# Pairs of the HGRN heads on column strips of the array, and a delta rule whose keys are transposed once for a pair of heads

## The chip, the cores and the metric

The kernel runs on one core of a Trainium2 chip. The metric is the device time of one execution in microseconds, from repeated runs. The profile is of one further execution. Its engines are PE (the matrix engine, TensorE), PEld (its weight loads), DVE (VectorE), ACT (ScalarE), POOL (GpSimd) and SP, which here only issues DMAs.

## What is computed

One layer of a diffusion backbone over 512 latent tokens and 256 context tokens of width 1024: a modulated norm, one input projection, two token mixers in parallel, their merge, an output projection, and a SwiGLU block. The change touches the two mixers. Both run in two directions over chunks of tokens:

```
# mixer A, gated delta rule, per chunk (u solved from a triangular system before)
u_c    = u_c - w_c @ s
s_next = gam_end * s + k_end.T @ u_c              # k_end = k * exp(g_end - g)
o      = (q * exp(g)) @ s + att @ u_c
# mixer B, HGRN2, per chunk
pair   = exp(lg[i] - lg[j])  for j <= i, else 0   # a decay per channel k
att_ij = sum_k q[i,k] * k[j,k] * pair[i,j,k]
o      = (q * exp(lg)) @ s + att @ v
```

## The kernel before

All matmuls of the wide projections are split in three products of rounded halves (line 110, a helper `mm3`; the halves `hi` and `lo` are made by ACT at line 100 and DVE at line 102). The order of all instructions on each engine is fixed when the program is built: a list `PLAN` says in which order steps of six streams are written down (two pairs of delta rule heads `G0` and `G2`, four HGRN heads `H0` to `H3`), with pieces of independent work between them (`F`, gate projections into `pgate`, and sums for the modulation), and a scheduler then interleaves them by priority. The rest of the gate projections is written behind the streams at a low priority, so that PE has it to fill gaps and to do at the end. Then come the up projections (`pup`), the output projection (`pwo`), and the SwiGLU block (`pf`, `pfo`).

**HGRN head (`hgrn`).** The decay of a pair in a chunk of 128 tokens can't be taken apart into a factor for i and one for j without overflow. So the pairs are split in a diagonal and seven levels b = 1, 2, 4, ... 64: at level b a pair is one whose two tokens lie in neighbouring halves of a block of 2b tokens. For each level `kq` holds scaled keys and queries (ACT lines 511 and 512, DVE line 513), and `att` (line 488) multiplies them for all 128 x 128 pairs of each of the 4 chunks into a PSUM bank `pA`; DVE (line 493) then copies only the pairs of that level into the matrix `AT`, by a mask `lev`. For the diagonal (level 7 in the code) ACT copies the whole product (line 491). K and L are moved on to the next level by DVE at lines 515 and 516. `AT` is used in the head's output `h_po`.

**Delta rule pair (`gdn_pair`).** Two heads (index e) are worked on together. A triangular system is solved in blocks of 32 and 64 (tiles `p_pR`, `p_pY`, `p_pX`, `p_pRb`, `p_pYb`, which are themselves matmuls on parts of the array), with `T1`, `T2` and `X64` as scratch in three buffers of the tag `blk`. Then six steps run over the chunks, with four independent states (two heads, two directions), each step in a PSUM bank `pk` out of three banks of the tag `ga`. A unit (one step of one state) is: keys times state (line 789), remainder `r` (DVE line 790), times the solved matrix (792), the update u = that product scaled by `nbkv` (ACT line 794), queries times state (796, latent chunks only), the transposed keys (799, PE against the identity) scaled by their decay to the end of the chunk into `ke` (ACT line 800), `ke` times u (801) into the new state (ACT line 804 in the first step, DVE line 806 later), and the output (810, ACT 815, DVE 813 and 816).

A product of 32-bit floats appears as two records on PE (two passes); a transposition against the identity as one. The products of rounded halves appear as one.

## Time and profile before

| | |
|---|---|
| time, median of 3 runs | 1084.16 us (1082.39 to 1086.25) |
| profiled execution, its own time | 1081.61 us |
| profiled execution, span from first to last instruction | 1079.6 us |
| mean granted TensorE clock | 0.990 of full |
| PE busy in the span | 1014.1 us (94%) |
| DVE busy | 656.5 us (61%) |
| ACT busy | 554.5 us (51%) |

The two mixers fill the span from about 100 to 580 us. The four heads make their pairs near 266 to 294, 345 to 386, 449 to 478 and 544 to 563 us, and the two pairs of delta rule heads step from 285.6 to 330.6 and from 471.2 to 513.5 us. A row of the timeline gives the start of a group of instructions, its length, and its count; the length holds the latency of the last one, so the spacing of a stream is read from starts.

### The profile page before, as it was taken

The numbers are of one execution on the slowest core, as the hardware profiler recorded it, in microseconds if no ns is written. First come the engines' busy times: TensorE is split into PE (matmuls) and PEld (weight loads), VectorE is DVE, ScalarE is ACT, GpSimd is POOL, SyncE is SP. The second block draws the span as 40 slices with busy tenths as digits, with TensorE's granted clock in tenths as the row PEclk, the third lists the DMA queues.
The fourth block names the chain that finished last, engine by engine and source line by source line (L and its number), as shares of the span: only waits on it lengthen the run. The fifth ranks groups of instructions, "written<-read, shape, count | busy, mean of one in ns | idle before, by whom it ended". The sixth has DMA issues, their size and how long they took to land.

```text
span 1079.6 us, 16501 instructions
## 1 busy us (share of the span) xinstructions
PE 1014.1 (94%) x6455; PEld 839.9 (78%) x6455; DVE 656.5 (61%) x1238; ACT 554.5 (51%) x1042; POOL 76.6 (7%) x133
## 2 busy tenths in 40 slices
PE   4999999979999999999999899999999999999996
PEld 2686788858897877789777688797888878888785
DVE  3336886789867967976797565776343433422524
ACT  3456578748976765887774643442222222221212
POOL 1010000320002022000201000010000000000000
PEclk8999999999999999999999999999999999999999
DMA  9953412122004213200738743455333323322222
GB/s 329 290 168 91 138 55 65 54 79 59 3 11 147 64 45 88 59 2 22 241 112 280 239 159 120 137 158 174 98 97 96 96 85 98 97 97 96 86 95 95
DMA packets 134529, 122.07 MB, mean 113 GB/s; under 512 B 5533, under 2 KB 110259, under 8 KB 134451
## 3 DMA queue, kind: packets, MB, share of 16 engines
q1 hardware_dynamic: 127715, 100.20, 29.9%
q0 software_dynamic: 4640, 17.30, 4.9%
q10 hardware_dynamic: 2096, 3.50, 0.9%
q8 instruction: 51, 0.84, 0.3%
q14 instruction: 27, 0.22, 0.1%
HBM read 110.51 MB, written 10.49 MB: 112 GB/s over the span
## 4 chain that ended last, share of the span: by engine, by line
PE 60%; DVE 13%; DMA 9%; ACT 7%; issue 7%; POOL 3%; SPq 0%; POOLq 0%; ACTq 0%; DVEq 0%
PE pf L110 20%; PE pfo L110 10%; PE pg L330 3%; PE pup L110 3%; PE h_z L110 3%; PE pgate L110 2%; DMA mwb<-in_mod_w_dram 2%; DVE lo L102 2%; DMA mwe<-in_mod_w_dram 2%; PE h_zv L110 2%; DMA ug<-gdram 1%; ACT hi L100 1%; DMA gdram<-gt 1%; PE p_s_pk L801 1%; PE g_k_zl L110 1%
## 5 line engine op out<-in xcount | busy, mean ns | idle before, releaser
L100 ACT CAST hi<-raw 128x1024 fp32r<-128x1024 f32 (+1 forms) x131 | 129.7, 991 | 279.9 <-PE pf L110 97.3
L102 DVE TENSOR_TENSOR lo<-raw,hi 128x1024 fp32r<-128x1024 f32 (+1 forms) x131 | 150.5, 1150 | 172.6 <-ACT hi L100 172.2
L110 PE MATMUL pf<-hhi,lo 128*128 128x512 f32 (+1 forms) x352 | 133.8, 380 | 0.8 <-DVE lo L102 0.8
L110 PE MATMUL pf<-hhi,hi 128*128 128x512 f32 (+1 forms) x352 | 133.8, 381 | 0.0
L110 PE MATMUL pf<-hlo,hi 128*128 128x512 f32 (+1 forms) x352 | 133.7, 380 | 0.0
L110 PEld LDWEIGHTS pf<-hhi,lo 128*128 128x128 f32 x352 | 66.2, 188 | 13.7 <-DVE lo L102 1.2
L110 PEld LDWEIGHTS pf<-hlo,hi 128*128 128x128 f32 x352 | 66.2, 188 | 12.5 <-DVE hlo L1042 0.2
L110 PEld LDWEIGHTS pf<-hhi,hi 128*128 128x128 f32 x352 | 66.1, 188 | 12.5
L110 PE MATMUL pfo<-lo,uh 128*128 128x512 f32 x176 | 68.8, 391 | 0.1
L110 PE MATMUL pfo<-hi,ul 128*128 128x512 f32 x176 | 68.5, 389 | 0.0
L110 PE MATMUL pfo<-hi,uh 128*128 128x512 f32 x176 | 67.9, 390 | 0.0
L110 PE MATMUL pgate<-hhi,lo 128*128 128x512 f32 x144 | 59.2, 412 | 6.5 <-DVE lo L102 6.5
L110 PE MATMUL pgate<-hhi,hi 128*128 128x512 f32 x144 | 59.2, 411 | 2.3 <-ACT hi L100 2.3
L110 PE MATMUL pgate<-hlo,hi 128*128 128x512 f32 x144 | 58.2, 404 | 0.0
L1098 DVE TENSOR_TENSOR sg<-sg,pf 128x512 f32<-128x512 f32 x22 | 15.1, 687 | 49.3 <-PE pf L110 49.3
L835 DVE SCALAR_TENSOR_TENSOR acc<-mwb,sc,acc 128x256 f32<-128x256 f32 x72 | 34.5, 484 | 12.4 <-DMA mwb<-in_mod_w_dram 11.2
L110 PEld LDWEIGHTS pfo<-lo,uh 128*128 128x128 f32 x176 | 33.0, 188 | 7.8 <-DVE lo L102 1.0
L110 PEld LDWEIGHTS pfo<-hi,uh 128*128 128x128 f32 x176 | 32.8, 188 | 7.4 <-ACT hi L100 0.7
L110 PEld LDWEIGHTS pgate<-hhi,lo 128*128 128x128 f32 x144 | 27.8, 193 | 13.8 <-DVE lo L102 8.9
L110 PE MATMUL h_z<-hhi,hi 128*128 128x512 f32 x96 | 38.1, 397 | 0.4 <-ACT abT L376 0.3
L110 PEld LDWEIGHTS pfo<-hi,ul 128*128 128x128 f32 x176 | 33.0, 188 | 6.8
L110 PE MATMUL h_z<-hhi,lo 128*128 128x512 f32 x96 | 38.0, 396 | 0.0
(443 smaller groups left out, 2498.3 us busy)
## 6 DMA issues: line engine op xcount, KB each, us to landing
raw<-in_ffn_w_in_dram SPq DMA_DIRECT2D x44, 512.0 KB, 3.7
raw<-in_w_in_dram SPq DMA_DIRECT2D x37, 512.0 KB, 3.7
raw<-in_ffn_w_out_dram SPq DMA_DIRECT2D x22, 512.0 KB, 3.6
mwb<-in_mod_w_dram POOLq DMA_DIRECT2D x18, 512.0 KB, 4.6
mw<-in_mod_w_dram SPq DMA_DIRECT2D x16, 512.0 KB, 6.0
mwe<-in_mod_w_dram POOLq DMA_DIRECT2D x7, 1024.0 KB, 6.1
gdram<-gt SPq DMA_DIRECT2D x24, 256.0 KB, 3.3
raw<-in_w_in_dram SPq DMA_DIRECT2D x18, 256.0 KB, 2.9
```

Of the source, the lines that this page charges most:

```text
L100: nc.scalar.copy(hi[:, :, :], raw[:, :, :])
L102: nc.vector.tensor_tensor(lo[:, :, :], raw[:, :, :], hi.bitcast(F32), op=ALU.subtract)
L110: nc.tensor.matmul(ps, a[u](k), b[v](k), start=(start and n == 0), stop=(stop and n == tot - 1))
L330: nc.tensor.matmul(pg0[i][:, :], u[:, P * i:P * i + P], v[:, d, :], start=(d == 0 and n == 0), stop=(d == KT - 1 and n == 2))
L801: nc.tensor.matmul(pk[:, 2 * P:3 * P], kend[:, :], u[:, :], start=True, stop=True)
L835: nc.vector.scalar_tensor_tensor(acc[:, :], mw[:, k - k0, :], sc[:, k:k + 1], acc[:, :], op0=ALU.mult, op1=ALU.add)
L1098: nc.vector.tensor_tensor(sg[:, :], sg[:, :], pgu[1][:, :], op=ALU.mult)
```

## The change

In the HGRN heads `att` no longer multiplies 128 x 128 pairs. For the diagonal and levels b = 1 to 16, all pairs of interest lie in diagonal blocks of 32 x 32, so 4 blocks a chunk are multiplied, each on its own strip of 32 columns of the array (`tile_position` (0, 32 j); all 128 rows are used, since the sum runs over 128 channels). Level 32 multiplies each block of 32 with its neighbour, in the same way; level 64 multiplies 2 blocks of 64 a chunk on strips of 64 columns. The product of a level so is 128 x 4 x 32 numbers instead of 128 x 4 x 128 (128 x 4 x 64 at level 64). The diagonal and the first five levels gather in a small tile `AD`, by a mask cut to 32 columns; four DVE copies put it into `AT`, and levels 32 and 64, of which every pair counts, go there by four and two ACT copies, without a mask.

In the delta rule, the six blocks of keys of a head are transposed ahead of the steps, in two PSUM banks of `ga`, and copied by ACT into a tile `kt` of the tag `blk`. The decay to the chunk's end is put on the update instead of the keys: `nbe` is `nbkv` times the decay, `ue` is the product scaled by `nbe`, and `kt` times `ue` gives the new state. u itself is made only for latent chunks, where the output needs it.

```diff
-    lev = [(r // (2 * b) == c // (2 * b)) & (r // b != c // b) for b in LEVELS]
+    r, c = r % NB, c[:, 0:NB]
+    lev = [(r // (2 * b) == c // (2 * b)) & (r // b != c // b) for b in LEVELS[0:NSM]]
...
             AT = hg.tile([P, 4, P], F32, name=n + "AT", tag="AT")
+            AD = hg.tile([P, 4, NB], F32, name=n + "AD", tag="AD")

             def att(kq, lvl):
+                w = 64 if lvl == 6 else NB
                 pA = bank("ha", f"{n}pA{lvl}")
                 for c in range(4):
-                    nc.tensor.matmul(pA[:, P * c:P * c + P], kq[:, 0, P * c:P * c + P], kq[:, 1, P * c:P * c + P],
-                                     start=True, stop=True)
+                    for j in range(P // w):
+                        kt0, qt0 = P * c + w * j, P * c + w * (j ^ (lvl in (5, 6)))
+                        nc.tensor.matmul(pA[w * j:w * j + w, w * c:w * c + w], kq[:, 0, kt0:kt0 + w], kq[:, 1, qt0:qt0 + w],
+                                         start=True, stop=True, tile_position=(0, w * j))
+                pAv = pA[:, 0:4 * w].rearrange("p (c i) -> p c i", i=w)
                 if lvl == 7:
-                    nc.scalar.copy(AT[:, :, :], pA.rearrange("p (c i) -> p c i", i=P))
+                    nc.scalar.copy(AD[:, :, :], pAv)
+                elif lvl < NSM:
+                    nc.vector.copy_predicated(AD[:, :, :], lev[:, NB * lvl:NB * lvl + NB].unsqueeze(1).to_broadcast([P, 4, NB]), pAv)
                 else:
-                    nc.vector.copy_predicated(AT[:, :, :], lev[:, P * lvl:P * lvl + P].unsqueeze(1).to_broadcast([P, 4, P]),
-                                              pA.rearrange("p (c i) -> p c i", i=P))
+                    for j in range(P // w):
+                        s = slice(w * j, w * j + w)
+                        nc.scalar.copy(AT[s, :, w * (j ^ 1):w * (j ^ 1) + w], pAv[s, :, :])
+                if lvl == NSM - 1:
+                    for j in range(P // NB):
+                        s = slice(NB * j, NB * j + NB)
+                        nc.vector.tensor_copy(AT[s, :, s], AD[s, :, :])
...
             oa2 = gd.tile([P, 2, 4, P], F32, name=n + "oa", tag="blk", bufs=3)
+            kts = []
+            for e, (KTt, QTt, Vt, nbkv, eq) in enumerate(heads):
+                kt = gd.tile([P, 6, P], F32, name=f"{n}kt{e}", tag="blk", bufs=3)
+                for g0, cnt in ((0, 2), (2, 4)):
+                    pt = bank("ga", f"{n}kt{e}{g0}")
+                    for i in range(cnt):
+                        nc.tensor.transpose(pt[:, P * i:P * i + P], KTt[:, g0 + i, :], ident)
+                    nc.scalar.copy(kt[:, g0:g0 + cnt, :], pt[:, 0:P * cnt].rearrange("p (g k) -> p g k", k=P))
+                nbe = gd.tile([P, 6, 2], F32, name=f"{n}nbe{e}", tag="nbe", bufs=2)
+                nc.vector.tensor_tensor(nbe[:, :, :], nbkv, dec[:, :, 1, :, h0 + e].rearrange("p d g -> p g d"), op=ALU.mult)
+                kts.append((kt, nbe))
...
                         u = rt
-                        nc.scalar.activation(u[:, :], pk[:, P:2 * P], AF.Copy, scale=nbkv[:, g, d:d + 1])
+                        if step < 5:
+                            kt, nbe = kts[e]
+                            ue = gd.tile([P, P], F32, name=m + "ue", tag="ke", bufs=3)
+                            nc.scalar.activation(ue[:, :], pk[:, P:2 * P], AF.Copy, scale=nbe[:, g, d:d + 1])
                         if g >= 2:
+                            nc.scalar.activation(u[:, :], pk[:, P:2 * P], AF.Copy, scale=nbkv[:, g, d:d + 1])
                             nc.tensor.matmul(pk[:, 3 * P:], QTt[:, g - 2, :], S[t][:, :], start=True, stop=True)
                         if step < 5:
-                            kend = gd.tile([P, P], F32, name=m + "ke", tag="ke", bufs=3)
-                            nc.tensor.transpose(pk[:, 2 * P:3 * P], KTt[:, g, :], ident)
-                            nc.scalar.activation(kend[:, :], pk[:, 2 * P:3 * P], AF.Copy, scale=dec[:, d, 1, g, h:h + 1])
-                            nc.tensor.matmul(pk[:, 2 * P:3 * P], kend[:, :], u[:, :], start=True, stop=True)
+                            nc.tensor.matmul(pk[:, 2 * P:3 * P], kt[:, g, :], ue[:, :], start=True, stop=True)
```

The program is scheduled anew, so instructions move. Two places matter. The first is PE at the start of the pairs of the first head (`h_pA` is the product of a level, `g_k_zl` a wide projection of the next delta rule head), before:

```order
L110 MATMUL g_k_zl<-hhi,lo_3505 128x512
L488 MATMUL h_pA_3125<-h_kqd 128x128 x4
L488 MATMUL h_pA_3136<-h_kq_3131 128x128 x4
L110 MATMUL g_k_zl<-hhi,hi_3503 128x512
L110 MATMUL g_k_zl<-hlo,hi_3503 128x512
L110 MATMUL g_k_zl<-hhi,lo_3505 128x512
```

and there in the changed program:

```order
L113 MATMUL g_k_zl<-hhi,lo_3600 128x512
L497 MATMUL h_pA_3124<-h_kqd 32x32 x16
L497 MATMUL h_pA_3147<-h_kq_3142 32x32 x16
L113 MATMUL g_k_zl<-hhi,hi_3598 128x512
L113 MATMUL g_k_zl<-hlo,hi_3598 128x512
L113 MATMUL g_k_zl<-hhi,lo_3600 128x512
L497 MATMUL h_pA_3172<-h_kq_3167 32x32 x16
L113 MATMUL g_k_zl<-hhi,hi_3598 128x512
```

Four matmuls of 128 x 128 became sixteen of 32 x 32, the next level comes three projections later instead of behind a block of solver matmuls, and the array goes from whole to strips and back. Over the program the stretches of instructions on parts of the array number 43 before and 64 now; 27 of the 64 hold pairs.

The second place is PE at the start of the steps of the first pair of delta rule heads (`p_pYb` is the end of the solver, `p_kt` the new transpositions, `p_s_pk` the units), before:

```order
L766 MATMUL p_pYb_2742<-p_N,p_T_2299 64x64 x6
L766 MATMUL p_pYb_2742<-p_N,p_T_2300 64x64 x6
L792 MATMUL p_s_pk<-p_s_r,p_N 128x128 x2
L488 MATMUL h_pA_3175<-h_kq_3170 128x128
L488 MATMUL h_pA_3188<-h_kq_3183 128x128 x2
L792 MATMUL p_s_pk<-p_s_r,p_N 128x128
L799 MATMUL p_s_pk<-sq,g_KT 128x128 x2
```

and now:

```order
L783 MATMUL p_pYb_2742<-p_N,p_T_2299 64x64 x6
L783 MATMUL p_pYb_2742<-p_N,p_T_2300 64x64 x6
L798 MATMUL p_kt_2773<-sq,g_KT 128x128 x2
L798 MATMUL p_kt_2777<-sq,g_KT 128x128 x4
L113 MATMUL g_k_zc<-chi,lo_3600 128x256
L113 MATMUL pgate_2393<-hhi,lo_2416 128x512
L497 MATMUL h_pA_3276<-h_kq_3271 32x32 x9
L798 MATMUL p_kt_2786<-sq,g_KT 128x128 x2
L497 MATMUL h_pA_3276<-h_kq_3271 32x32 x7
L113 MATMUL g_k_zc<-chi,hi_3598 128x256
```

The transpositions of both heads stand ahead of the first units, with projections and pairs between them. The matching copies on ACT now stand ahead of the first update:

```order
L799 COPY p_kt_2772<-p_kt_2773 128x256
L799 COPY p_kt_2772<-p_kt_2777 128x512
L799 COPY p_kt_2785<-p_kt_2786 128x256
L507 COPY h_AT<-h_pA_3276 32x4x32
L799 COPY p_kt_2785<-p_kt_2790 128x512
L826 ACTIVATE p_s_ue<-p_s_pk,p_nbe_2783 128x128 x2
```

In the second pair of heads the twelve transpositions stand with only the eight matmuls of one level between them, and no projection.

## Rows read from the trace of the kernel before

**Rows 1.** The page: busy time of each engine, and the granted clock in 40 slices.

```profile
PE 1014.1 (94%) x6455; PEld 839.9 (78%) x6455; DVE 656.5 (61%) x1238; ACT 554.5 (51%) x1042; POOL 76.6 (7%) x133
...
PEclk8999999999999999999999999999999999999999
```

**Rows 2.** Windows: stretch, its length, busy of PE, PEld, DVE, ACT, POOL; clock, DMA.

```profile
250.00:300.00 50.00, 47.17 (x602) 41.01 (x601) 43.72 (x88) 43.71 (x99) 1.12 (x6) 1.00 0.12 33
...
525.00:570.00 45.00, 42.43 (x280) 36.03 (x280) 40.90 (x76) 32.87 (x53) 3.75 (x5) 1.00 0.51 159
...
475.00:515.00 40.00, 39.70 (x303) 36.66 (x302) 26.61 (x79) 29.81 (x92) 3.38 (x4) 1.00 0.09 29
578.00:600.00 22.00, 22.00 (x99) 18.23 (x98) 14.23 (x23) 13.77 (x20) 0.75 (x1) 1.00 0.90 295
```

**Rows 3.** Timeline of PE where the last gates end and the up projection begins.

```profile
599.84 0.39 PE L110 MATMUL pgate<-hhi,lo 128*128 128x512 f32 x1
600.07 0.39 PE L110 MATMUL pup<-yh,hi 128*128 128x512 f32 x1
```

**Rows 4.** Waits of PE from 250 to 580 us: total, times, longest.

```profile
PE p_pR L735 <- DVE p_T L703: 2.8, 2, 1.5
...
PE h_pA L488 <- ACT h_kqd L501: 0.9, 2, 0.7
```

**Rows 5.** The tile h_pA: instructions, duration in ns (least, median, most).

```profile
L488 PE MATMUL h_pA<-h_kq x224: 270/275/377, 266.8 to 563.0; 128*128 128x128 f32 x112
...
L488 PE MATMUL h_pA<-h_kqd x32: 270/275/377, 265.9 to 544.7; 128*128 128x128 f32 x32
L493 DVE COPY_PREDICATED h_AT<-lev,h_pA x28: 694/736/755, 270.6 to 563.3; 128x512 f32<-128x512 uint8 x28
L491 ACT COPY h_AT<-h_pA x4: 569/586/586, 267.0 to 545.1; 128x512 f32<-128x512 f32 x4
```

**Rows 6.** Timeline of PE around a group of 32 x 32 matmuls and one level.

```profile
270.79 0.62 PE L735 MATMUL p_pR<-p_T,p_N 32*32 32x32 f32 x48 [1.30 <-DVE p_T L703]
...
272.03 1.13 PE L488 MATMUL h_pA<-h_kq 128*128 128x128 f32 x8
272.92 0.48 PE L110 MATMUL g_k_zl<-hhi,hi 128*128 128x512 f32 x1
```

**Rows 7.** The tile g_k_pn, sums on strips; ns.

```profile
L116 PE MATMUL g_k_pn<-ones,g_k_acc x192: 170/170/191, 133.6 to 346.9; 128*32 128x1 f32 x192
```

**Rows 8.** Timeline of PE around sums on strips of 32 columns.

```profile
133.28 0.39 PE L110 MATMUL pgate<-hlo,hi 128*128 128x512 f32 x1
133.60 0.58 PE L116 MATMUL g_k_pn<-ones,g_k_acc 128*32 128x1 f32 x48
134.10 0.50 PE L110 MATMUL g_k_zl<-hhi,hi 128*128 128x512 f32 x1
```

**Rows 9.** Timeline of PE, four strips that stream 512 columns each.

```profile
27.75 1.06 PE L279 MATMUL pmod<-mw,sch 128*32 128x512 f32 x8
```

**Rows 10.** Timeline of PE around matmuls on quarters of 64 x 64.

```profile
280.04 0.91 PE L760 MATMUL p_pRb<-p_X,p_N 64*64 64x64 f32 x24
280.88 0.39 PE L110 MATMUL g_k_zc<-clo,hi 128*128 128x256 f32 x1
```

**Rows 11.** The tile p_s_pk: count, duration in ns.

```profile
L794 ACT ACTIVATE p_s_r<-p_s_pk,g_vec x48: 352/368/402, 286.7 to 511.9; 128x128 f32<-128x128 f32 x48
L799 PE MATMUL p_s_pk<-sq,g_KT x40: 270/273/331, 287.1 to 505.8; 128*128 128x128 f32 x40
...
L816 DVE TENSOR_TENSOR p_oa<-p_oa,p_s_pk x32: 276/286/289, 301.0 to 513.5; 128x128 f32<-128x128 f32 x32
...
L804 ACT COPY p_s_S<-p_s_pk x8: 256/266/313, 288.7 to 477.8; 128x128 f32<-128x128 f32 x8
```

**Rows 12.** Copies of a part of the partitions (tile p_pY); ns.

```profile
L750 ACT COPY p_N<-p_pY x16: 292/310/312, 276.6 to 467.2; 32x192 f32<-32x192 f32 x16
```

**Rows 13.** Waits of DVE from 250 to 580 us: total, times, longest.

```profile
DVE p_s_S L806 <- PE p_s_pk L801: 7.7, 16, 0.8
```

More of the change, by code (lines that the diff above doesn't have):

```diff
@@ L26 @@
 LEVELS = (1, 2, 4, 8, 16, 32, 64)
+NB = 32
+NSM = 5
 PADN = 8 * 68 + 260
@@ L342, in body @@
             columns(1)
-            lev = cp.tile([P, 7 * P], U8, name="lev")
-            levf = s1.tile([P, 7 * P], F32, name="levf")
+            lev = cp.tile([P, NSM * NB], U8, name="lev")
+            levf = s1.tile([P, NSM * NB], F32, name="levf")
             nc.sync.dma_start(levf[:, :], T["lev"])
```

## The prediction

> **What bounds the kernel now.** I read the busy shares first. PE is busy for 1014.1 of 1079.6 us and runs at full granted clock but for the very start [rows 1]. Busy time of PE holds the latency of pipelined matmuls, so I asked next whether the stages that the change touches are full. In the window of the first head's pairs PE is busy 47.17 of 50 us, but DVE also 43.72 and ACT 43.71; beside the fourth set of pairs the shares are 42.43, 40.90 and 32.87 of 45. In the steps of the second delta rule pair PE has 39.70 of 40 and DVE only 26.61 [rows 2]. So PE leads everywhere, with DVE close behind beside the pairs. Last I asked what happens with PE time that comes free. From 578 us, when the last head is done, PE works off gate projections without a break until 599.84, and the up projection starts at 600.07 [rows 2, 3]. This backlog of 22 us may be done at any earlier time. Whatever PE is spared before 578 us therefore moves everything behind it forward, unless PE waits instead. It does wait at places in these stages, but the items are small: 2.8 us for DVE before the solver's matmuls is one of the largest, 0.9 us for ACT before the pairs [rows 4].
>
> **PE time of the pairs before.** Each level makes 8 records; on PE they take 272.92 - 272.03 = 0.89 us, 0.111 us each [rows 6]. There are 224 + 32 = 256 records [rows 5]: 256 x 0.111 = 28.5 us.
>
> **PE time of the pairs after.** The trace has no record with 128 rows, a strip of 32 columns and 32 moving columns, but three neighbours. Sums on strips (128 rows, 32 columns, one moving column) last 0.17 us each [rows 7]; 48 of them take 0.58 us together, so their starts lie within 0.41 us, 8.7 ns apart [rows 8]. On 32 x 32 blocks with 32 moving columns, 48 records take 0.62 us, 12.9 ns each with the last one's latency in it [rows 6]. On strips of 32 columns with 512 moving, 8 records take 1.06 us, 0.13 each; by the column that is 8 ns for 32 [rows 9]. All are near 9 ns, the strips running beside each other. Seven of the eight levels of four heads have 32 records each: 896 x 9 ns = 8.1 us. Level 64 has 4 x 16 = 64. On 64 x 64 quarters 24 records held PE for 280.88 - 280.04 = 0.84 us with the exit [rows 10]; less 0.09 for that (next paragraph) 31 ns each, two at a time: 2.0 us.
>
> Changing between the whole array and strips costs too. The strips of the sums begin 133.60 - 133.28 = 0.32 us after a matmul that holds PE for 0.23, so 0.09 late; the next whole one begins at 134.10, some 0.09 after the last strip's start at 133.60 + 0.41 = 134.01, of which 0.01 is its own [rows 3, 8]. That is 0.17 us for a visit. The order of the new program has 64 visits where there were 43: 21 x 0.17 = 3.6 us. Sum 8.1 + 2.0 + 3.6 = 13.7, so **14.8 us of PE are saved**. The other end: if strips did not overlap with 32 moving columns, a record might hold PE for the 31 ns of [rows 10]; then 896 x 31 ns = 27.8 us, and with 2.0 and 3.6 the pairs would cost 4.9 us more than before. I take the 9 ns, because the two neighbours on the same strips bracket the case in moving columns (1 and 512).
>
> A rule speaks against this. The Trainium skill, page "TensorE: Matmul & The Clock Gate", section "Wait — 56ns, not 53.3ns?", says that starts of matmuls never come closer than about 25 ns, however few columns. By it the 960 records would need at least 24 us, and with the visits hardly 1 us of the saving would be left. This trace disagrees where it can be asked: 48 records on strips start within 0.41 us [rows 8].
>
> **Delta rule on PE.** 40 transpositions of one record [rows 11] become 24: 16 x 0.11 = **1.8 us saved**.
>
> **DVE.** 28 masked copies of 0.736 us (20.6 us, [rows 5]) become 20 of a quarter of the width. A DVE operation of 128 columns from PSUM takes 0.286 [rows 11]; by pure proportion it would be 0.18. I take 0.3: 6.0 us. The copies of `AD` into `AT`, 16 of 128 numbers in 32 partitions, are put at 0.25 (bounds 0.1 and 0.29): 4 us. The four `nbe` are 24 columns or less per partition and vanish. DVE is spared **10 us**, 2.5 us a head.
>
> **ACT.** A head trades a copy of 0.586 for 0.266 at the diagonal [rows 5, 11], and gets four copies of 32 partitions (0.310 for 192 columns, so about 0.28 for 128, [rows 12]) and two of 256 columns (between 0.31 and 0.59, say 0.4): +1.6 us a head, +6.4 in all. In the delta rule 48 + 40 scalings of 0.368 (the 40 are as many as the transpositions, [rows 11]) become 32 + 40: -5.9. The copies of `kt` are eight, four of 256 columns (0.4) and four of 512 (0.59): +4.0. ACT gains work by some 4.5 us; it is the least busy of the three over these stages, and costed at nothing while PE or DVE is what is waited for. If it were the bound, these 4.5 us would be the price.
>
> **Start of the steps.** The two sets of `kt` copies, 2 x (0.4 + 0.59) = 2.0 us a pair, stand on ACT ahead of the first update, and the transpositions use banks of `ga` that the first units need. Before, the first unit followed the solver at once. In the first pair projections are written between, so I charge 0.5 us; in the second there is only one level of pairs, so I charge the whole 2.0. Together **2.5 us lost** (bounds 0 and 4).
>
> **Inside a unit.** The new state needs product, `ue`, matmul; before it needed product, u and also `ke`, both on ACT, which stood in either order. The state's path has lost up to one ACT operation of 0.37 us, and the output's path has got one, since u now stands behind `ue`. In 32 latent units the bank may be held 0.37 us longer; three banks share this, so at most 32 x 0.37 / 3 = 4 us. DVE waited 7.7 us for PE before the state's update, in 16 cases [rows 13], and PE is full there [rows 2], so I put it at nothing and keep 4 us for the range.
>
> **Sum.** PE: 14.8 + 1.8 = 16.6 saved, 2.5 lost at the start of the steps: 14.1. Beside the pairs DVE is nearly as full as PE and is spared only 10 us over the heads. A stage that DVE ended would give that much, one that PE ended the whole. Between 10 and 14.1, with a little less waiting, I take **13 us**. The profiled execution's 1081.61 us would become about 1068.6. It was 2.5 us quicker than the median of the runs, 1084.16; against that median I predict **1071 us**.
>
> **Rivals.**
> *The chains set the pace (about 1078).* The levels of a head are a chain of ACT, DVE, PE and DVE work. If that and the solver end the stages, PE's spared time turns into waiting, and only half of the 13 us is seen. For it: DVE at 43.72 of 50. Against it: PE's small waits, and the backlog after 578 us.
> *All of it and more (about 1064).* PE's 16.6 us come out whole and the relief on DVE also removes waits before solver matmuls, 20 us in all. For it: the 2.8 us for DVE in [rows 4].
> *Hidden (about 1083).* The spared time is lost again at the start of the steps and in the units (4 + 4 us) and in the chains. It needs every bound at its bad end.
> *Strips in turn (about 1090, slower).* The strips do not run beside each other with 128 rows and 32 moving columns of 32-bit floats; a record holds PE for 31 ns. Pairs cost 4.9 us more, the transpositions give 1.8 back, the start of the steps takes 2.5: 1084.2 + 5.6. It decides from (28.5 + 1.8 - 2.0 - 3.6 - 2.5) / 896 = 25 ns a record on. Against it: [rows 8, 9]. The 25 ns that the Trainium skill's page "TensorE: Matmul & The Clock Gate" names would end just there, at no change; since [rows 8] contradict it, it has no more than a part of this case's chance.
>
> **How the numbers follow.** Main case, 9 to 17 us faster, 1067 to 1075: 0.57. Chains: 0.18. All and more: 0.10. Hidden: 0.07. Strips in turn, with any other loss: 0.08. A change of 0.3%, 3.3 us, is about what a measurement of this kernel can tell from none. The first three cases lie beyond it: faster 0.85, same 0.07, slower 0.08. The range takes the main case, most of the chains and of the larger gain: 1062 to 1080.
>
> **What the next profile shows.** Right, if groups of 16 matmuls on `h_pA` (32 records) take about 0.3 us and the following whole matmul starts within 0.45 us of the first strip; if the masked copies take about 0.3 us; and if the up projection starts some 13 us before 600. The strips are wrong if a level still holds PE for 0.9 us or more. The step about the backlog is wrong if `h_pA` is short but the up projection starts less than 7 us earlier: then DVE or ACT ends the waits before the pairs and the solver. The start of the steps is wrong if PE stands idle for more than 2 us between the end of the solver and the first unit. What would overturn all of it: a new order in which PE waits in turn for short copies on a busy ACT.

## The result and the profile after

| | before | after |
|---|---|---|
| time, median of 9 runs each, taken together | 1082.39 us (1078.73 to 1086.25) | 1091.93 us (1088.95 to 1094.69) |
| ratio after to before | | 1.0094, 95% [1.0074, 1.0114] |
| profiled execution: own time, span | 1081.61, 1079.6 | 1094.69, 1093.0 |
| mean granted TensorE clock | 0.990 | 0.972 |

The change made the kernel 9.5 us slower, where 13 us faster were predicted. Its page, beside [rows 1]:

```profile
span 1093.0 us, 17930 instructions
...
PE 1017.6 (93%) x7143; PEld 833.3 (76%) x7143; DVE 645.9 (59%) x1250; ACT 557.4 (51%) x1058; POOL 76.4 (7%) x133
...
PEclk8999999989999999999898899999999999999998
```

DVE lost 10.6 us of work and ACT gained 2.9. PE's busy time did not fall, although its records need 21 us less (the table below); it holds the time at half clock too. The clock's digit, 9 in all slices but the first before, is now 8 in 6. The windows that answer to [rows 2], the last three moved with their work:

```profile
250.00:300.00 50.00, 46.18 (x762) 37.36 (x762) 40.95 (x85) 43.52 (x92) 1.12 (x6) 1.00 0.18 49
535.00:580.00 45.00, 39.11 (x410) 30.96 (x410) 38.85 (x76) 34.88 (x58) 3.00 (x4) 0.88 0.50 155
484.00:517.00 33.00, 31.77 (x238) 28.97 (x238) 20.98 (x65) 22.60 (x79) 1.01 (x1) 1.00 0.06 17
592.00:612.00 20.00, 20.00 (x87) 16.07 (x87) 11.98 (x21) 13.46 (x20) 0.80 (x1) 1.00 0.91 299
```

Beside the fourth set of pairs PE now idles for 6 of 45 us (2.6 before), and its clock there is 0.88. The backlog of gates behind the last head is still 20 us. The tile of the pairs, with its idle time, against [rows 5]:

```profile
L497 PE MATMUL h_pA<-h_kq x832: 189/196/369, 269.0 to 572.8; 128*32 128x32 f32 x154, 128*64 128x64 f32 x13
...
L497 PE MATMUL h_pA<-h_kqd x128: 196/196/243, 268.7 to 555.9; 128*32 128x32 f32 x128
L507 ACT COPY h_AT<-h_pA x24: 237/258/367, 292.9 to 574.3; 32x128 f32<-32x128 f32 x16, 64x256 f32<-64x256 f32 x8
L503 DVE COPY_PREDICATED h_AD<-lev,h_pA x20: 279/300/311, 270.0 to 567.3; 128x128 f32<-128x128 uint8 x20
...
  DVE h_kq L530: 8.9, 8
  issue: 6.5, 12
  ACT h_kqd L518: 6.0, 4
```

The strips do what was predicted: 960 records, each starting 7 ns (median) behind the last. The masked copy takes 0.300 us. What is new is the idle time in front, until DVE's factor of a level (`h_kq`) or ACT's factor of the diagonal (`h_kqd`) is there. The last three rows count PE and its weight loads, so a wait can stand in them twice. PE alone, from 250 to 592 us (against [rows 4], where `h_kq` of DVE has no row):

```profile
PE h_pA L497 <- DVE h_kq L530: 6.6, 5, 2.7
...
PE h_pA L497 <- ACT h_kqd L518: 2.3, 1, 2.3
```

PE's timeline at the solver of the second pair, in the last head, and where the up projection starts (against [rows 3, 6]):

```profile
466.02 0.62 PE L752 MATMUL p_pR<-p_T,p_N 32*32 32x32 f32 x48 [1.16 <-DVE p_T L720]
...
526.23 0.28 PE L113 MATMUL h_z<-chi,lo 128*128 128x256 f32 x1
530.17 0.47 PE L440 MATMUL p_pt<-sq,p_on 128*128 128x128 f32 x1 [3.66 <-ACT p_on L437]
...
566.74 0.46 PE L497 MATMUL h_pA<-h_kq 128*32 128x32 f32 x32
569.85 0.46 PE L497 MATMUL h_pA<-h_kq 128*32 128x32 f32 x32 [2.66 <-DVE h_kq L530]
571.96 1.12 PE L497 MATMUL h_pA<-h_kq 128*64 128x64 f32 x16 [1.65 <-DVE h_kq L530]
...
611.65 0.39 PE L113 MATMUL pgate<-hhi,lo 128*128 128x512 f32 x1
611.88 0.39 PE L113 MATMUL pup<-yh,hi 128*128 128x512 f32 x1
```

In this stretch a level of 32 records holds PE for 0.46 us with its latency, and then PE has nothing until the next, 2 to 3 us later. Windows (columns as in [rows 2]) over two such waits and the stretch behind each:

```profile
526.00:530.00 4.00, 0.51 (x5) 0.30 (x3) 3.71 (x10) 0.35 (x2) 2.72 (x2) 1.00 0.35 123
530.00:536.80 6.80, 6.63 (x39) 5.78 (x40) 3.83 (x9) 3.86 (x9) 1.20 (x2) 0.50 0.56 195
567.00:571.00 4.00, 0.66 (x58) 0.46 (x44) 3.65 (x10) 1.97 (x5) 0.00 (x0) 1.00 0.19 72
571.00:581.20 10.20, 8.21 (x42) 6.75 (x42) 8.61 (x17) 6.54 (x17) 1.12 (x2) 0.50 0.34 103
```

PE worked 0.5 to 0.7 of 4 us, DVE nearly all of it; then the granted clock was 0.50, its lower level of 1.2 GHz, for 6.8 and 10.2 us. The Trainium skill ("TensorE: Matmul & The Clock Gate", section "What's actually happening") says that the engine falls to that level when it was idle. This trace agrees in these two stretches.

**Where the 13 us of span went.** I split PE's span by the start times of its records: a record's slot at full clock, what was longer at half clock, up to 0.095 us for each change between array and strips, and the rest as waiting. (A few short records overlap, so a row sums to 3 to 5 us over the span. The profiled execution is the longest of the nine, so 13 us here stand for 9.5 between the medians.)

| us | slots | half clock | changes | waiting |
|---|---|---|---|---|
| before | 952.3 | 6.2 | 7.7 | 118.3 |
| after | 931.2 | 19.8 | 11.5 | 133.5 |
| after - before | -21.1 | +13.6 | +3.8 | +15.2 |

PE was spared 21 us. Against them stand 15 us of waiting, nearly 14 lost at half clock and 4 for changes of the array's mode.

By place, in starts of PE's records: the first pair's steps end where they did (328.7 us, 328.9 before), the second pair's solver starts 8.9 us later (466.0, 457.1 before), the last record of its steps stands 5.9 later (518.6), the last head's 13.5 later (591.4, 577.9 before). So the loss lies in the stretches with the heads, ahead of the second solver and behind its steps, and the steps themselves give time back.

### The profile page after: what moved, and what is told of

Its sections match the earlier page's. It is cut to its first block, busy times and chain, and to the rows that moved or that the text cites. A ratio compares the mean times of both kernels' runs of the same rounds, so it can differ in the third digit from the quotient of the medians.

```text
span 1093.0 us, 17930 instructions
## 1 busy us (share of the span) xinstructions
PE 1017.6 (93%) x7143; PEld 833.3 (76%) x7143; DVE 645.9 (59%) x1250; ACT 557.4 (51%) x1058; POOL 76.4 (7%) x133
## 4 chain that ended last, share of the span: by engine, by line
PE 41%; DVE 5%; ACT 4%; DMA 3%; issue 3%; POOL 1%; SPq 0%; POOLq 0%; ACTq 0%; DVEq 0%
PE pf L113 20%; PE pfo L113 10%; PE pup L113 4%; PE pgate L113 1%; DVE lo L105 1%; PE pwo L113 1%; PE h_z L113 1%; DMA mwb<-in_mod_w_dram 1%; DMA ug<-gdram 1%; ACT hi L103 1%; DMA uy<-ydram 1%; DMA raw<-in_ffn_w_in_dram 0%; PE p_s_pk L821 0%; PE p_s_pk L818 0%; DMA raw<-in_w_out_dram 0%
## 5 line engine op out<-in xcount | busy, mean ns | idle before, releaser
L865 DVE SCALAR_TENSOR_TENSOR acc<-mwb,sc,acc 128x256 f32<-128x256 f32 x72 | 33.9, 480 | 11.8 <-DMA mwb<-in_mod_w_dram 10.7
L113 PE MATMUL h_z<-hlo,hi 128*128 128x512 f32 x96 | 38.3, 399 | 0.0
```

What stands on the lines that cost most here:

```text
L113: nc.tensor.matmul(ps, a[u](k), b[v](k), start=(start and n == 0), stop=(stop and n == tot - 1))
L865: nc.vector.scalar_tensor_tensor(acc[:, :], mw[:, k - k0, :], sc[:, k:k + 1], acc[:, :], op0=ALU.mult, op1=ALU.add)
```

## The experiments

The theory (A) after the result: PE's time doesn't end these stages. A head's levels are a chain on ACT and DVE, and spared PE time turns into waiting, with the clock falling behind it. Rivals: the strips themselves lose (mode, clock); the part with the keys loses; or the new order of the program does. Each ratio is to the kernel before on the same chip.

**The two parts alone.** `e1_pairs` has the strips and their copies with the delta rule of before, `e2_keys` the reverse.

> Only the pairs on strips; the delta rule is as before. Theory A (PE's spared time turns into waiting between short levels, and the granted clock falls after such waits): slower than the kernel before by 5 to 14 us, with at least 20 us more at half clock than the 24 us of before, most of it beside the pairs. Theory B (strips of 32 columns do not hold the clock, whatever is waited for) says the same here. Theory C (the keys' part of the change costs the time): within 3 us of before, or faster.

> Only the keys transposed once for a pair of heads and the updates scaled; the pairs are as before. Theory A and B: the same or faster by up to 8 us, with half-clock time within 10 us of before. Theory C: slower by 5 to 10 us, with PE waiting at the start of the steps and ahead of the head norm.

Measured: 1091.83 us, 1.009 [1.006, 1.012], and 1086.13 us, 1.0041 [1.0024, 1.0058]. The pairs alone came out as A and B had it in time and at half clock (45.8 us, 24.3 before), though only part of that lies beside the pairs; the keys alone came out between A and C. Both lose, and together they lose no more than the pairs alone. With the keys alone the delta rule's steps, from the first to the last product with the solved matrix, took 34.7 and 34.2 us where they had taken 42.1 and 40.2, and still the up projection started at 605.8 instead of 600.1 us. A stage got 6 to 7 us shorter and the program longer: the first sign that a stage's own length does not decide the time here.

**Strips without their gain, and the changed kernel with PE filled up.**

```diff
 e3_wide, on the kernel before: four strips that move all 128 columns; copies as before
+                    for j in range(0, P, 32):
+                        nc.tensor.matmul(pA[j:j + 32, P * c:P * c + P], kq[:, 0, P * c + j:P * c + j + 32], kq[:, 1, P * c:P * c + P],
+                                         start=True, stop=True, tile_position=(0, j))
 e4_pad, on the changed kernel: four more products behind each level, into unused columns
+                for i in range(4):
+                    nc.tensor.matmul(pA[:, 256:512], hhi[:, i, 0:P], hhi[:, i, 0:256], start=True, stop=True)
```

> The kernel before, with each level's 128 x 128 products issued as four strips of 32 columns that each move all 128 columns of the chunk: the same products, the same copies, about the same PE time a level (0.9 us) and a visit to strips for each level. Theory A: 2 to 6 us slower than before, which is the changing between array and strips (about 30 visits at 0.17 us), and half-clock time within 7 us of before. Theory B: new stretches at half clock beside the pairs, 15 us or more, and slower by 8 us or more.

> The changed kernel, with four products of 128 x 128 by 256 columns, whose result nobody reads, behind the strips of every level: 128 records of about 0.12 us, 15 us of added PE work that brings a level back to about 0.9 us. Theory A: the stretches at half clock beside the pairs go, and in spite of the added work the time is 2 to 12 us below that of the changed kernel. A theory by which only the order and the chains count, and the clock is no cause (D): no faster than the changed kernel, up to 15 us slower. Theory B: clock partly restored, time within 5 us of the changed kernel.

`e3_wide`: 1102.43 us, 1.019 [1.0164, 1.0216]. Its pairs took 3 us more PE time than before (28.5 us between the starts of a group's records, 25.3 before), with 31 more visits to strips, and yet it lost 20 us, far more than A had it. It spent 42.5 us at half clock, 18 more than before, 7 of them behind the last pairs; that comes near B, so this run does not clear the strips. `e4_pad`: 1094.15 us, 1.0119 [1.009, 1.0148], 2 to 3 us over the changed kernel (the intervals overlap) for about 15 us of added products, where A had it faster by 2 to 12. In its profile the clock was as before (7.2 us lost at half clock, against 19.8) and waiting fell to 125.7; the mean clock of all its executions is 0.984 to 0.990. So the clock can be kept by work between the levels, and the time doesn't come back with it. That is what D had forecast, by which order and chains count and the clock is no cause; A's part on the clock missed.

**Gates between the levels; their weights on GpSimd; their products without a lag.**

```diff
 e5_ride, on the changed kernel: four gates kept for the last head, in the order of the code
-F:1 G2:99 N:1 H3:99 aT:1 H2:1 X H2:99"
+F:1 G2:99 N:1 H3:99 aT:1 H2:1 X F:1 H2:4 F:1 H2:2 F:1 H2:2 F:1 H2:99"
 e8_pool, on the changed kernel: low halves of the gates' weights
-            nc.vector.tensor_tensor(lo[:, :, :], raw[:, :, :], hi.bitcast(F32), op=ALU.subtract)
+            (eng or nc.vector).tensor_tensor(lo[:, :, :], raw[:, :, :], hi.bitcast(F32), op=ALU.subtract)
 e11_prio, on the changed kernel
-                tc.cur_priority += 1000
+                tc.cur_priority += 0
```

> The changed kernel, with four of the gate projections that stood behind the last head written between the levels of that head (each 24 products of 0.227 us, 5.4 us of PE). Theory A (PE's spared time turns into waits between short levels, since the order holds no other work there): the waits between the levels of the last head are filled, the stretches at half clock at 571 and 622 us go, and the up projection starts 5 to 12 us earlier than in the changed kernel: about 1080 to 1087. Rival (the head's chain on DVE and ACT ends this stage, and the gates' weights, split on the same two engines, lengthen it as much as the backlog shrinks): within 3 us of the changed kernel, 1089 to 1095.

> The changed kernel, with the low halves of the gates' weights (two of 0.93 us on DVE for each of the 16 gates written beside the heads and the delta rule, some 30 us of DVE) made on GpSimd, which is nearly idle there. If the amount of DVE's work sets the pace of these stages, 10 us or more faster than the changed kernel, 1078 to 1083. If the chain of single operations or PE's order does (theory A), 0 to 5 us faster, 1087 to 1092; slower if GpSimd's own duration delays the gates: up to 1100.

> The changed kernel, with the products of the gates that are written between the heads no longer held back behind all work of the heads (their place in the queue is that of the code, no lag); nothing else is changed. If it is the order on PE, with the gates falling at the wrong places, that loses the spared time, this moves it, up or down, by more than 3 us: outside 1089 to 1095. If the chain of the levels and of the solver ends the stages in any order: inside.

`e5_ride`: 1094.84 us, 1.0128 [1.0105, 1.0151]. The backlog behind the last head shrank from 20.5 to 9.7 us, but the stretch from the second delta rule to the last head's end grew from 74.0 to 81.7. In the profile the up projection started 5.7 us earlier than in the changed kernel's, the stretch behind it was 3.0 us longer (484.1 against 481.1), and over all its executions the kernel is no faster, as the rival had it. `e8_pool`: 1102.23 us, 1.0203 [1.018, 1.0225], slower than any of its forecasts. DVE was relieved of 21 us and not of the 30 expected; a low half of 512 columns took 1.29 us on GpSimd (median) against 0.69 on DVE, and DVE's operations beside it got longer (line 711: 0.401 us against 0.329). `e11_prio`: 1097.39 us, 1.0126 [1.0097, 1.0156], on the slow side of the 1089 to 1095 by which the gates' order would not matter (the interval overlaps that of the change). In these three runs, filling PE's gaps with useful work or relieving DVE did not help either.

**PE time added and taken away in the kernel before.** `e10_single` is the cleanest of all runs: the instructions of before stand in the same order, row for row on PE and DVE (on ACT four copies have become casts). `F32R` stores the factors of the pairs rounded, so that a product is one record and not two: half the records of the pairs are gone.

```diff
 e6_twice
-                for c in range(4):
+                for c in (0, 1, 2, 3, 0, 1, 2, 3):
 e10_single
-            kq = hg.tile([P, 2, SEQ], F32, name=n + "kqd", tag="kq", bufs=2)
+            kq = hg.tile([P, 2, SEQ], F32R, name=n + "kqd", tag="kq", bufs=2)
```

> The kernel before, with every level's eight products made twice (256 more records of 0.111 us, 28.5 us of PE; the output is unchanged). If PE's time ended the stages with the heads before, as the prediction had it, the time rises by about as much as the prediction had it fall per us: 25 to 29 us, to 1108 to 1112. If chains on DVE and ACT end them (theory A), PE's waits of these stages take up half or more: 1085 to 1097.

> The kernel before, with the same 128 products of the pairs on the whole array, but their two factors stored as fp32r, so that each is one record of 128 columns instead of two (the attention of the HGRN heads is rounded by it; nothing is left out). PE and DVE have the instructions of before in the same order; copies, chains and the array's mode are those of before. From the 0.111 us of a record before and 0.227 for 512 columns of fp32r, a product falls from 0.22 to about 0.06: PE is spared some 21 us, as much as the strips spare. If PE's spared time comes out at the end (the prediction's step), 10 to 21 us faster than before: 1061 to 1072. Theory A (it turns into waits of PE for the chain on DVE and ACT between levels, and the granted clock falls after such waits): 0 to 6 us faster, 1076 to 1083, PE's waits up by 15 us or more.

`e6_twice`: 1108.99 us, 1.0256 [1.0233, 1.0279]: 28.0 us for 28.5 of added PE time (in a remade order). That is what the prediction's step had forecast, and not A. `e10_single`: 1081.14 us against 1081.52, 0.9991 [0.9973, 1.001]. That is what A had forecast, and not the prediction's step. Its records still start 0.11 us apart, so 14 us were spared and not 21; that is about what the strips spare when their changes of mode are taken off (between the starts of a group's records the pairs held PE for 10.8 us, 10.4 with strips, 25.3 before). PE's timeline of `e10_single`, in the order of the solver, a level and the up projection:

```profile
456.50 0.62 PE L735 MATMUL p_pR<-p_T,p_N 32*32 32x32 f32 x48 [1.94 <-DVE p_T L703]
...
563.27 0.64 PE L488 MATMUL h_pA<-h_kq 128*128 128x128 f32 x4
563.74 0.30 PE L542 MATMUL h_pk<-sq,h_K 128*128 128x128 f32 x1
...
600.94 0.39 PE L110 MATMUL pgate<-hhi,lo 128*128 128x512 f32 x1
601.16 0.39 PE L110 MATMUL pup<-yh,hi 128*128 128x512 f32 x1
```

And its windows, where those of [rows 2] stand:

```profile
250.00:300.00 50.00, 44.94 (x570) 38.39 (x569) 42.44 (x88) 42.21 (x99) 0.90 (x2) 0.97 0.08 23
525.00:570.00 45.00, 40.40 (x248) 32.66 (x247) 40.17 (x76) 33.08 (x53) 3.17 (x5) 0.98 0.51 161
475.00:515.00 40.00, 39.63 (x300) 36.32 (x299) 26.60 (x78) 30.00 (x91) 3.12 (x4) 1.00 0.08 26
```

Half as many records, and every place stands within 3 us of where it stood before: the level costs 0.47 instead of 0.89 us, the solver starts at 456.5 (457.1 before), the up projection at 601.2 (600.1). Slots fell by 14.2 us, waiting rose by 11.0 and the loss at half clock by 2.5, without any strip. PE's waits of over 0.15 us between 250 and 580 us sum to 26.1 us, 18.3 before. Two rows of them, where those of [rows 4] stand:

```profile
PE p_pR L735 <- DVE p_T L703: 4.1, 2, 2.2
...
PE h_pA L488 <- DVE h_kq L513: 1.3, 3, 0.8
```

PE now waits longer for DVE ahead of the solver (2.8 us before) and between levels (no such row before). This shows A's first half: in the order of before, PE time taken from the pairs is worth nothing (by the interval at most 3 us of 14). Together with `e6_twice` it reads as a knee, with PE and the chains of ACT and DVE about equally long: more PE work costs time, less gives none. The costly side is argued and not shown, since `e6_twice` has another order as well.

**A shorter chain.** In a level DVE updates K, then L, and the next level's first exponential waits for L. Here L goes first (a few edge values are copied ahead).

```diff
+                    nc.vector.tensor_copy(le[:, :, 0:m], view(L[:, 1, :], 2 * b - 1, [(1 - 2 * b - TOK, 2), n2b]))
+                    nc.vector.tensor_tensor(Lv, Lv, view(L[:, 0, :], b, [(TOK - 1, 2), n2b, (0, b)]), op=ALU.add)
+                    nc.vector.tensor_tensor(Kv, Kv, Le, op=ALU.subtract)
```

> The changed kernel, with the chain from level to level shortened for the four levels from 8 to 64: the update of L, on which the next level's first exponential waits, stands before the update of K instead of behind it (the few edge values that K needs of the old L are copied first, 0.07 to 0.15 us on DVE). No work is taken from any engine. Theory A (the chain of a level, L update, exponential, product on DVE, sets the pace, whatever PE does): up to 0.69 less 0.1 us per level, 16 levels, 9 us at most, 4 to 9 us faster than the changed kernel: 1083 to 1088. If the sum of DVE's or PE's work sets the pace, or the written order alone: 1090 to 1095.

> The kernel before, with the update of L ahead of that of K in the levels 8 to 64, as in the experiment on the changed kernel that had it (5 us faster there); no work is taken from an engine. If the chain of a level, on DVE and ACT, ends these stages in the kernel before too (theory A in its strong form), 4 to 6 us faster than before: about 1076 to 1079. If PE's work ends them there (the kernel before rose by 28.0 us when 28.5 us of PE were added), no change: within 2 us of before.

> The part with the keys alone (1.0041 of before by itself), with the update of L ahead of that of K in the levels 16 to 64. If a shorter chain is worth 1.4 us a level-set of a head here as in the changed kernel (5 us for 16 levels): 12 levels, about 3 to 4 us, 1082 to 1083. If the kernel with whole-array pairs is bound by PE there: no change, 1085 to 1087.

On the changed kernel (`e7_lfirst`) 1086.13 us, 1.005 [1.0032, 1.0068], about 5 us better than the change. On the kernel before (`e9_blf`) 1082.61, 0.9992 [0.9965, 1.0019]: nothing. On the keys alone (`e12_keys_lf`) 1096.21, 1.0122 [1.0095, 1.0149]: 9 us worse than without, by the ratios. Nearly the same edit (on the keys alone it leaves out level 8) is worth -5, 0 and +9 us. So A's strong form, that one chain sets the pace everywhere, fails. With each edit the program is ordered anew, and the order seems to outweigh the edit.

**What of the order.** DVE's timeline of the changed kernel in the recursion of the second pair's solver (lines 711 and 713):

```profile
457.02 0.30 DVE L503 COPY_PREDICATED h_AD<-lev,h_pA 128x128 f32<-128x128 uint8 x1
457.21 0.27 DVE L713 TENSOR_TENSOR p_Z<-p_Z,p_o 128x108 f32<-128x108 f32 x1
457.40 0.69 DVE L533 TENSOR_TENSOR h_L<-h_L 128x512 f32<-128x512 f32 x1
458.00 0.24 DVE L711 TENSOR_TENSOR p_o<-p_Z 128x84 f32<-128x84 f32 x1
458.19 0.69 DVE L532 TENSOR_TENSOR h_K<-h_K,h_L 128x512 f32<-128x512 f32 x1
458.80 0.24 DVE L713 TENSOR_TENSOR p_Z<-p_Z,p_o 128x84 f32<-128x84 f32 x1
458.96 0.69 DVE L530 TENSOR_TENSOR h_kq<-h_q,h_E 128x512 f32<-128x512 f32 x1
```

Between any two steps shown here stands an operation of the third head's levels. Inside the recursion's 60 operations there are 14 of these, 6 before: levels that come ready earlier get in front of the solver. From the first to the last start of a product (line 711) it lasts 37.3 us (423.4 to 460.7), 33.7 before. `e13_hold` holds the levels back, `e14_hold_b` does so in the kernel before, `e15_hold_lf` adds the shorter chain.

```diff
-            lk = lno[:, h:h + 1]
+            lk = held[0] if h == 3 else lno[:, h:h + 1]
...
+            if h0 == 2:
+                lk3 = cp.tile([P, 1], F32, name="lk3")
+                nc.vector.scalar_tensor_tensor(lk3[:, :], Z[:, 31, 0:1], 0.0, lno[:, 3:4], op0=ALU.mult, op1=ALU.add)
+                held.append(lk3[:, :])
```

> The changed kernel, with the levels of the third head in time (H3) held until the recursion of the second pair's solver is done on DVE: the bias of its exponentials is written behind the recursion. In DVE's order of the changed kernel 14 operations of that head's levels stand inside the 60 of the recursion, where there were 6 before; now none does. If the changed kernel loses there (theory A, made narrower: levels that come ready earlier get in front of the solver on DVE), the recursion takes 5 to 9 us less, the solver's products start 4 to 8 us earlier, and 3 to 8 us of it come out: 1084 to 1089. Rivals (clock and array mode alone, or the chain of the levels): the products start earlier, but the levels end as much later, and the time stays within 2 us: 1089 to 1094.

> The same hold in the kernel before, as a control: 6 operations (about 4 us of DVE) leave the recursion. If theory A is right for the changed kernel, the gain here is half as large or nothing, 0 to 4 us: 1077 to 1082. If a hold is worth as much here as there, it says nothing about the change.

> The changed kernel with this hold and with the update of L ahead of that of K for the levels 8 to 64 (5 us faster by itself). If the two losses are apart (solver behind levels, chain of the levels), they add: 1078 to 1084, as fast as before or faster. If they are the same waiting seen twice: 1084 to 1088.

`e13_hold`: 1089.6 us, 1.0062 [1.0039, 1.0086], 2 to 4 us better than the change (the intervals overlap), between A's forecast and the rivals'. `e14_hold_b`: 1088.25, 1.0053 [1.0031, 1.0075], 6 us worse than before and outside its forecast; its solver's products started 5.1 us earlier than before (452.0) and its up projection 8.5 later (608.6). `e15_hold_lf`: 1093.44, 1.0113 [1.0087, 1.0139], outside both of its forecasts: the two gains neither add nor stay. DVE's and PE's timelines of `e13_hold`:

```profile
450.02 0.22 DVE L711 TENSOR_TENSOR p_o<-p_Z 128x58 f32<-128x58 f32 x1
450.27 0.22 DVE L713 TENSOR_TENSOR p_Z<-p_Z,p_o 128x58 f32<-128x58 f32 x1
450.53 0.19 DVE L711 TENSOR_TENSOR p_o<-p_Z 128x30 f32<-128x30 f32 x1
450.75 0.19 DVE L713 TENSOR_TENSOR p_Z<-p_Z,p_o 128x30 f32<-128x30 f32 x1
```

```profile
456.25 0.62 PE L756 MATMUL p_pR<-p_T,p_N 32*32 32x32 f32 x48 [0.94 <-DVE p_T L724]
...
607.18 0.40 PE L113 MATMUL pup<-yh,hi 128*128 128x512 f32 x1
```

The recursion took 30.4 us, and the solver's products started 9.8 us earlier than in the changed kernel's profile (466.02). Of that, 3.1 us are only that profile's late start (its first solver's products began at 274.2 us, here at 271.1, with the same order up to there); 6.7 are the hold's. At the up projection 1.6 of them are left (611.88 - 3.1 - 607.18). The displacement is real in its place, but most of what the hold wins there is lost again in later work.

**Short copies without strips.** One product on the whole array for the strips of a chunk, on the changed kernel (`e16_whole`) and with the delta rule of before (`e17_whole_p`).

```diff
-                    for j in range(P // w):
-                        kt0, qt0 = P * c + w * j, P * c + w * (j ^ (lvl in (5, 6)))
-                        nc.tensor.matmul(pA[w * j:w * j + w, w * c:w * c + w], kq[:, 0, kt0:kt0 + w], kq[:, 1, qt0:qt0 + w],
-                                         start=True, stop=True, tile_position=(0, w * j))
+                    nc.tensor.matmul(pA[:, w * c:w * c + w], kq[:, 0, P * c:P * c + P], kq[:, 1, P * c:P * c + w],
+                                     start=True, stop=True)
```

> The changed kernel without strips: a level of a chunk is one product on the whole array, 128 columns of the one factor by the first 32 (64 in level 64) of the other, in place of the strips; all copies and the part with the keys are those of the change. What it leaves out: of each chunk's diagonal blocks only the first is right. PE is spared about as much as by the strips (8 records of some 0.11 us at most for a level, no change of the array's mode). If it is the strips themselves that lose (the array's mode and the clock after them), the time comes back: 1076 to 1084. If the short copies, the order and the chain lose, with PE's time worth nothing (theory A): 1084 to 1094.

> The same without strips, with the delta rule as it was before (the counterpart of the kernel with the strips alone, 1.009 of before). It leaves out the same. Strips themselves lose: 1076 to 1083. Order, short copies and chain: 1084 to 1094.

1095.02 us, 1.0127 [1.0105, 1.0149], and 1098.63, 1.0158 [1.0131, 1.0185]: no faster than the same kernels with strips, and above both forecasts. A level of `e16_whole` on PE:

```profile
564.87 0.97 PE L495 MATMUL h_pA<-h_kq 128*128 128x32 f32 x8
565.68 0.48 PE L113 MATMUL pgate<-hhi,hi 128*128 128x512 f32 x1
```

A record of 32 moving columns on the whole array holds PE as long as one of 128, 0.11 us, so PE is not spared here, against what I expected. But there are no strips in the pairs, the changes of mode are nearly those of before (8.3 us), and the loss is still there; the clock too was at half for 55.9 us in `e16_whole`, 63.2 in the changed kernel, 24.3 before. So neither the loss nor the half clock needs strips. That strips cost nothing is not shown: their changes of mode took 3.8 us.

## Why the prediction was wrong

**The step that failed** is "Whatever PE is spared before 578 us therefore moves everything behind it forward, unless PE waits instead", and the sum built on it. `e10_single` spares 14 us in the same order and moves the up projection by +1.1 us. I had looked at PE's waits, found them small, and took the 22 us of gates behind the last head as work that would fill what comes free. But small waits can also mean that PE's work and the chains are of about equal length. And the order on each engine is written at the build: a gate fills a gap only where it stands in it. The backlog was 22 us and is 20. The prediction had named the sign: `h_pA` short (32 strips start within 0.26 us, the next whole matmul 0.39 us behind the first) and the up projection less than 7 us earlier. It came 11.8 us later. The reading of [rows 1] was wrong as well: a digit stands for 27 us, and the kernel before was at half clock for 24.3 us, 10.2 of them in three stretches between 84 and 232 us.

**The terms.** The pairs on PE: 14.8 us spared as predicted, some 15.6 measured: 25.3 - 10.4 between the starts of a group's records, 4.5 for the last record of each of the 40 groups before, less 3.8 for changes of mode. The records start 7 ns apart, not 9, against the 25 ns of the Trainium skill's page "TensorE: Matmul & The Clock Gate", section "Wait — 56ns, not 53.3ns?". DVE: 10 predicted, 10.6 measured. ACT: +4.5 predicted, +2.9 measured. The delta rule's 16 transpositions fewer: right.

```profile
L798 PE MATMUL p_kt<-sq,g_KT x24: 272/273/332, 290.1 to 483.7; 128*128 128x128 f32 x24
L799 ACT COPY p_kt<-p_kt x8: 372/495/607, 291.9 to 484.0; 128x256 f32<-128x256 f32 x4, 128x512 f32<-128x512 f32 x4
```

The start of the steps was mis-sized: 2.5 us charged, while from the solver's first product to the first unit it took 14.8 and 14.1 us before, 18.9 and 17.8 after, 7.8 us more (5.4 with the keys alone). PE idled for at most 0.6 us between the solver's last product and the first unit, so the prediction's sign for this did not show; PE had other work there, and the first unit came 3.1 us behind that product, 0.15 before. Inside the units I put nothing; the steps became 7.7 and 6.7 us shorter. So every other term came out about as priced or better, and the sum has the wrong sign.

**The rivals.** "The chains set the pace" had the right mechanism, PE's spared time turning into waiting, but priced it at half the gain left. "Strips in turn" landed closest in time for a reason that the trace refutes. The last sentence of the prediction, a new order in which PE waits in turn, names part of what the runs point to, and had no chance of its own; but PE's largest waits in the changed kernel are for DVE's factor of a level (6.6 us) and for ACT ahead of a head norm (6.2 us, `p_on`), and only 0.6 us for the short copies on ACT that it names.

**Why slower, and not equal.** Of the kernels with a remade order, one was as fast as before (`e9_blf`) and all others 0.4 to 2.6% slower, with strips or without, with PE spared, equal or added. `e14_hold_b` has, but for one tiny operation, exactly the work of before, and loses 0.5%; but it adds a wait to one head, and its executions spread from 1080.6 us to 1091.3, so it shows that an order with one added wait can cost this much, and not yet that an order alone can. That a remade order costs the 9.5 us here is the reading that fits most runs; it isn't shown. No run has the change's work in the order of before, or the work of before in another order and nothing else. Open is how much of the 13.6 us at half clock would remain in a better order, which displacements behind the solver give its gain back, and whether an order exists in which the changed program is faster. None of 17 kernels beat the kernel before.

## What to carry to other kernels

An engine that is 94% busy beside two that are 87% busy, as PE is here beside the first pairs, may stand at a knee: adding to it costs, taking from it gives nothing. Before rebuilding its work, take the time away in a way that keeps every instruction in its place (here another number format) and see whether anything moves. Where a program is ordered anew at each build, compare several orders before crediting or blaming an edit of 1%.

## What the hardware showed that was not expected

- Strips of 32 columns with 128 rows and 32 moving columns start 7 ns apart, while on the whole array 32 moving columns hold PE as long as 128, 0.11 us.
- The granted clock fell to 0.50 in the middle of the program as well; the two stretches shown stand behind waits of PE. Over the whole program it stood there for 63.2 us in the changed kernel and 24.3 before, and for 31.6 in `e10_single`, without strips in the pairs.
- A subtraction of 512 columns takes 1.29 us on GpSimd (median of 18) against 0.69 on DVE, and DVE slows beside it (0.329 to 0.401 us for line 711).
